# The last two rows of a decoder's last product: residual added in the PSUM bank, both parts of an input in one wide product, stores of two rows

## The chip, the cores and the metric

The kernel runs on one core of a Trainium2 chip. The metric is the device time of one execution in microseconds, the median of three runs. Engines are called TensorE (PE in the profile, with PEld for its weight loads), VectorE (DVE), ScalarE (ACT), GpSimd (POOL) and SyncE (SP).

## What is computed

A decoder of two layers on 512 tokens of width 1024 in fp32; the change touches only the very end: the down projection of the second layer's feed-forward block, the residual, and the final norm.

```python
def rms_norm(x, g):
    xf = x.astype(jnp.float32)
    y = xf * lax.rsqrt(jnp.mean(xf * xf, axis=-1, keepdims=True) + EPS)
    return (y * g.astype(jnp.float32)).astype(x.dtype)

def swiglu(h, w_gate_up, w_down):
    gu = h @ w_gate_up
    return (jax.nn.silu(gu[..., :D_FF]) * gu[..., D_FF:]) @ w_down

# in reference(), per layer and at the end:
        x = x + swiglu(rms_norm(x, ln_ffn[layer]), w_gate_up[layer], w_down[layer])
    ...
    return rms_norm(x, ln_final)
```

## The kernel before

Everything is held transposed: `self.x[m]` is one of eight rows of the residual, 128 features (the partitions) by 512 tokens. A product in nearly fp32 precision is made of three passes: each operand is split into a high and a low part (`split`, `pair`), and `mm3` issues weight-high times input-high, weight-high times input-low and weight-low times input-high into one PSUM bank. The two parts of an input are two tiles, `h` and `l`.

The feed-forward block works in two halves of 11 feature tiles. At its end `acts` holds 11 pairs of inputs, and for each row m a product of 11 times `mm3` is made over two weight pieces (`w[m][0]` of six tiles, `w[m][1]` of five), which are fetched through two buffers (`wraw`) and split by ScalarE (high) and VectorE (low). Rows 0 to 5 of the last product are 512 tokens wide: VectorE adds the bank to the residual (`add`), ScalarE squares the row, and VectorE adds the square to the running total (`accumulate`).

Rows 6 and 7 are made in the branch `if tail < KD`, for each half of the tokens apart (`parts`), so that the first half can be normed and sent while the second is still computed. The order there is: row 6 of the first half, row 7 of the first half, row 6 of the second, row 7 of the second. Ahead of them in the program, ScalarE scales rows 0 to 5 of both halves by the final gain into output tiles (`outs`, tag `T`): twelve instructions. After each of the four units VectorE adds the bank to the residual, ScalarE squares; row 6 is scaled into its output tile. `final` then sums the squares over the partitions with two products by ones (into a bank `g`), and ScalarE takes the reciprocal root twice, to the bank and to SBUF. `store` multiplies: rows 0 and 1 on GpSimd, rows 2 and 3 and then rows 4 to 6 on VectorE, row 7 on VectorE with the gain in the same instruction; each piece is sent as soon as it is done, three by SyncE's queue and rows 0 and 1 of the second half by ScalarE's.

The banks of the products rotate: `pj` has two, so row 6 of the first half takes the bank that row 4 had, and row 7 the one that row 5 had. Each engine works through its own instructions in order, and a wait holds up all that stands behind it on that engine.

Of the kernel before, what the change touches and what calls it, by code (L numbers as in the profile page):

```python
# [10 lines left out]
F32R = mybir.dt.float32r  # L11
I32 = mybir.dt.int32
AF = mybir.ActivationFunctionType
ALU = mybir.AluOpType
# [4 lines left out]
P = 128  # L19
T = 512  # L20
D = 1024
KD = D // P
# [17 lines left out]
G_MIX, G_FFN, G_KV, G_FIN = (0, 8), (16, 24), 32, 40  # L40
# [43 lines left out]
    return c  # L84


class Builder:
    def __init__(self, tc, a):
        self.tc, self.nc, self.a = tc, tc.nc, a
        self.n = 0  # L90
        self.valued, self.turned, self.scaled, self.behind = None, [], None, None
        self.scalings = []
        self.table, self.table_ins, self.table_users = None, None, []
# [67 lines left out]

    def pair(self, pool, tag=None, bufs=None):
        if tag is None:
            tag, bufs = "", KD
        return tuple(self.t(pool, [P, T], F32R, tag + p, bufs) for p in "hl")


    def split(self, src, hi, lo, eng=None):
# [27 lines left out]
    def mm3(self, ps, w, k, act, start, stop, more=False):  # L196

        (wh, wl), (ah, al) = w, act
        s = slice(k * P, (k + 1) * P)
        self.head = self.mm(ps, wh[:, s], ah, start, False, more)  # L200
        self.mm(ps, wh[:, s], al, False, False, more)
        self.last = self.mm(ps, wl[:, s], ah, False, stop, more)

    def project(self, src, acts, tag="pj", order=range(KD), w=None):
        steps = self.projected(src, acts, tag, order, w)
        return list(steps)[-1]
# [887 lines left out]
    def ffn(self, fp, xp, layer, h, apool, rope=False):  # L1094

        nc, a = self.nc, self.a
        acc = self.acc
        half = FT // 2
        acts, sums, open_pairs, places, waiting = [], [], [], [], []
# [52 lines left out]
        def add(x, ps):  # L1152
            d = ps
            if not layer:
                d = self.t(fp, [P, T], F32, "fu", 3)
                self.tt(nc.vector, d, ps, self.rstd, ALU.mult)
            self.tt(nc.vector, x, d, x, ALU.add)

        for f0 in (0, half):
# [22 lines left out]
            for m in range(tail):  # L1182
                if layer and f0 == 0:
                    self.tt(nc.vector, self.x[m], self.x[m], self.root, ALU.mult)
                ps = self.bank("pj")
                for j, n in ((0, 6), (6, 5)):
                    w = down(m, j, n)
# [7 lines left out]
        if tail < KD:  # L1195

            parts = (slice(0, T // 2), slice(T // 2, T))
            own = dict(pool=fp, tags=("T", "T"), bufs=8)
            w = {m: [down(m, j, n, **(own if m == KD - 1 else {})) for j, n in ((0, 6), (6, 5))] for m in range(tail, KD)}
            outs = [[self.t(fp, [P, D], F32, "T", 8).rearrange("p (k t) -> p k t", k=4) for _ in range(2)] for t in parts]  # L1200
            for o, t in zip(outs, parts):
                for k in range(tail):
                    self.copy(o[k // 4][:, k % 4, :], self.x[k][:, t], scale=self.gain(G_FIN, k))
            ends = []
            for t in parts:
                acc = self.acc[:, t]
                for m in range(tail, KD):
                    ps = self.bank("pj")[:, t]
                    for k in range(half):
                        self.mm3(ps, w[m][k // 6], k % 6, [x[:, t] for x in acts[k]], k == 0, k == half - 1)  # L1210
                    x = self.x[m][:, t]
                    add(x, ps)
                    sq = self.t(fp, [P, T], F32, "fg", 4)[:, t]
                    self.square(sq, x)
                    if m < KD - 1:
                        self.copy(outs[len(ends)][1][:, m % 4, :], x, scale=self.gain(G_FIN, m))
                        nxt = self.t(xp, [P, T], F32, "sqa", 2)[:, t]
                        self.tt(nc.vector, nxt, acc, sq, ALU.add)
                        acc = nxt
                ends.append(self.final(fp, (acc, sq), t))  # L1220
            for n, ((ps, r), o, t) in enumerate(zip(ends, outs, parts)):
                self.store(ps, r, o, t, n)

    def token_sums(self, fp, layer, j, h):

# [269 lines left out]
            self.fn(o, ps, AF.Abs_reciprocal_sqrt, scale=1.0 / D)  # L1495
        return to, r

    def store(self, ps, r, o, t, part):

        nc = self.nc  # L1500
        rows = self.a["out"][part]
        some = lambda k, n: o[k // 4][:, k % 4:k % 4 + n, :]
        wide = lambda f, n: f.unsqueeze(1).to_broadcast([P, n, t.stop - t.start])
        send = lambda k, n, by=nc.sync: by.dma_start(rows[:, k:k + n, :], some(k, n))
        self.tt(nc.gpsimd, some(0, 2), some(0, 2), wide(r, 2), ALU.mult)
        for k, n in ((2, 2), (4, 3)):
            self.tt(nc.vector, some(k, n), some(k, n), wide(ps, n), ALU.mult)
            send(k, n)
        self.stt(some(7, 1)[:, 0, :], self.x[7][:, t], self.gain(G_FIN, 7), ps, ALU.mult, ALU.mult)
        send(7, 1)  # L1510
        send(0, 2, nc.scalar if part else nc.sync)


def layout(i):
# [30 lines left out]
    for k in range(0, KD, 2):  # L1545
# [7 lines left out]
        "wmk": wmk[1], "wmv": wmv[1],  # L1553
        "wout": np.stack([tiles(wo[0]), tiles(o1)]),
        "wgu": np.stack([tiles(w, pair) for w in gu]),
        "wdn": np.stack([tiles(w) for w in f("w_down")]),
        "wkv": tiles(f("w_kv")),
# [18 lines left out]
```

## Time and profile before

| | |
|---|---|
| time of the runs, median | 1139.19 us (1138.91 to 1139.49) |
| profiled execution, its time | 1139.24 us |
| its span | 1137.2 us |
| granted TensorE clock | 0.999 |
| TensorE busy | 99% of the span |
| the four tail units and what follows | from 1111.17 us to the end |

The profile follows one execution. A row of the timeline has start, length, engine, line, operation, output and inputs, shape and count, and in brackets how long the engine was idle before and what ended that. Most instructions have the line of a helper: L146 is a product, L140 a ScalarE copy or scaling, L143 a square, L153 a VectorE or GpSimd operation on two tensors, L134 a function of ScalarE, L156 a VectorE operation with a scalar. Products are pipelined: the distance of two starts tells what one takes, not its length. `x12` is twelve merged instructions.

### The profile page before, as it was taken

Reading aid. Unit: us, or ns where it says so; the run is one execution under the profiler, and the core shown is the slowest. Engines: PE = TensorE matmul, PEld = TensorE weight load, DVE = VectorE, ACT = ScalarE, POOL = GpSimd, SP = SyncE. Lnnn points to the kernel's source line nnn. Section 1 sums busy time; section 2 is a strip of 40 time slices with the busy share of each in tenths; the row PEclk is TensorE's granted clock in tenths of the full one; section 3 lists DMA queues with packets and bytes.
Section 4 is the critical chain, followed back from the end, with each engine's and each line's share of the span. In section 5 each row is a group of like instructions: output and inputs, shape, how many; then the busy total and the mean of one; then the engine's idle time right before and its main releaser. Section 6 shows DMA issues by size and latency. Waiting matters only on the chain.

```text
span 1137.2 us, 19289 instructions
## 1 busy us (share of the span) xinstructions
PE 1127.4 (99%) x7337; PEld 991.3 (87%) x7337; DVE 829.0 (73%) x1542; ACT 634.1 (56%) x1271; POOL 72.8 (6%) x89
## 2 busy tenths in 40 slices
PE   9999999999999999999999999999999999999997
PEld 8888778887899988899988887788999988999986
DVE  7676976577888975588955877839999533889543
ACT  8588664566566632366643555956666322666433
POOL 0000000000011001011000000000112000111000
PEclk9999999999999999999999999999999999999999
DMA  8344352244677536378433421116677533776232
GB/s 312 116 145 149 93 130 85 84 121 148 172 163 187 142 108 176 106 178 200 126 89 101 130 74 38 56 39 194 142 203 182 141 100 105 171 191 154 78 101 86
DMA packets 71536, 151.14 MB, mean 133 GB/s; under 512 B 16861, under 2 KB 17141, under 8 KB 71445
## 3 DMA queue, kind: packets, MB, share of 16 engines
q1 hardware_dynamic: 60164, 129.21, 36.7%
q0 software_dynamic: 11136, 20.45, 11.5%
q8 instruction: 57, 0.93, 0.3%
q14 instruction: 35, 0.28, 0.1%
q10 hardware_dynamic: 144, 0.26, 0.1%
HBM read 142.94 MB, written 6.96 MB: 132 GB/s over the span
## 4 chain that ended last, share of the span: by engine, by line
PE 95%; DVE 2%; ACT 1%; DMA 1%; issue 0%; DVEq 0%; SPq 0%; ACTq 0%
PE pj L146 45%; PE g L146 38%; PE sc L146 6%; PE qk L146 3%; PE pt L146 2%; PE pt L150 1%; PE g L150 1%; DVE big L153 1%; ACT T L140 0%; DVE wlo L153 0%; DVE qv L156 0%; DVE btmp L153 0%; DMA early<-in_early 0%; ACT sm L134 0%; DMA wraw<-in_wdn 0%
## 5 line engine op out<-in xcount | busy, mean ns | idle before, releaser
L140 ACT ACTIVATE whi<-wraw 128x512 fp32r<-128x512 f32 (+3 forms) x318 | 235.9, 749 | 253.5 <-PE pj L146 167.6
L153 DVE TENSOR_TENSOR wlo<-wraw,whi 128x512 fp32r<-128x512 f32 (+3 forms) x318 | 263.3, 838 | 92.4 <-ACT whi L140 84.8
L146 PE MATMUL pj<-h,whi 128*128 128x512 f32 (+1 forms) x652 | 256.4, 395 | 0.0
L146 PE MATMUL pj<-l,whi 128*128 128x512 f32 (+1 forms) x652 | 254.4, 390 | 0.0
L146 PE MATMUL pj<-h,wlo 128*128 128x512 f32 (+1 forms) x652 | 254.1, 390 | 0.0
L146 PE MATMUL g<-T,whi 128*128 128x256 f32 x1216 | 218.5, 280 | 0.0
L146 PEld LDWEIGHTS g<-T,whi 128*128 128x128 f32 x1216 | 186.1, 188 | 1.2 <-DVE fu L156 1.2
L146 PE MATMUL g<-T,wlo 128*128 128x256 f32 x608 | 170.1, 280 | 0.0
L146 PEld LDWEIGHTS pj<-h,whi 128*128 128x128 f32 x652 | 122.4, 188 | 28.2 <-issue 4.1
L146 PE MATMUL g<-h,wlo 128*128 128x256 f32 (+1 forms) x500 | 146.1, 292 | 0.0
L146 PE MATMUL g<-l,whi 128*128 128x256 f32 (+1 forms) x500 | 146.0, 292 | 0.0
L146 PE MATMUL g<-h,whi 128*128 128x256 f32 (+1 forms) x500 | 145.6, 291 | 0.0
L146 PEld LDWEIGHTS pj<-h,wlo 128*128 128x128 f32 x652 | 122.5, 188 | 25.3 <-issue 0.9
L146 PEld LDWEIGHTS pj<-l,whi 128*128 128x128 f32 x652 | 122.8, 188 | 24.0 <-DVE l L1444 0.3
L146 PEld LDWEIGHTS g<-T,wlo 128*128 128x128 f32 x608 | 114.3, 188 | 0.0
L146 PEld LDWEIGHTS g<-l,whi 128*128 128x128 f32 x500 | 95.0, 190 | 2.0
L146 PEld LDWEIGHTS g<-h,whi 128*128 128x128 f32 x500 | 94.9, 190 | 2.0
L146 PEld LDWEIGHTS g<-h,wlo 128*128 128x128 f32 x500 | 95.1, 190 | 1.7
L1262 POOL DMA_DIRECT2D ws<-in_wgu x38 | 33.5, 881 | 741.2 <-DMA ws<-in_wgu 584.6
L140 ACT ACTIVATE whi<-ws 128x512 fp32r<-128x512 f32 x76 | 48.0, 632 | 47.1 <-PE g L146 37.8
L153 DVE TENSOR_TENSOR wlo<-ws,whi 128x512 fp32r<-128x512 f32 x76 | 52.1, 685 | 6.9 <-ACT whi L140 6.8
L1263 POOL DMA_DIRECT2D ws<-in_wgu x38 | 34.4, 906 | 194.4 <-DVE wlo L153 92.2
(399 smaller groups left out, 1681.4 us busy)
## 6 DMA issues: line engine op xcount, KB each, us to landing
wraw<-in_wgu SPq DMA_DIRECT2D x50, 512.0 KB, 4.2
ws<-in_wgu SPq DMA_DIRECT2D x76, 256.0 KB, 3.4
ws<-in_wgu POOLq DMA_DIRECT2D x76, 256.0 KB, 4.8
wraw<-in_win SPq DMA_DIRECT2D x26, 512.0 KB, 3.7
wraw<-in_wdn SPq DMA_DIRECT2D x32, 384.0 KB, 3.1
wraw<-in_wdn SPq DMA_DIRECT2D x32, 320.0 KB, 2.9
wraw<-in_wgu SPq DMA_DIRECT2D x38, 256.0 KB, 4.4
wraw<-in_wout SPq DMA_DIRECT2D x16, 512.0 KB, 3.5
```

The lines of the kernel that those rows point to most:

```text
L140: self.copied = self.nc.scalar.activation(out, in_, AF.Copy, **kw).ins
L146: return self.nc.tensor.matmul(out, lhsT, rhs, start=start, stop=stop, skip_group_check=more).ins
L150: return self.nc.tensor.transpose(out, in_, self.ident[:k, :k]).ins
L153: return eng.tensor_tensor(out=out, in0=a, in1=b, op=op).ins
L1262: nc.gpsimd.dma_start(s1, a22, accum_op=ALU.add)
L1263: nc.gpsimd.dma_start(s3, a21, accum_op=ALU.add)
```

## The change

The two parts of an input become one tile of 128 x 2 x 512 (`pair`), so that a product can read both for the same tokens. In the tail, ScalarE first copies the residual into the unit's own half of the bank. For three of the four units it also writes zeros into the other half (`clear`: ones times 0.0), and `wide` takes the weight's high part against both parts of the input in one product of 2 x 256 columns, which adds into both halves, and the weight's low part against the input's high part into the own half. Afterwards ScalarE copies the low half out, and VectorE adds it to the own half. The last unit (row 7, second half) takes the three passes of 256 columns as before, onto the residual in its bank; its square and its scaled row are read from the bank. `store` sends rows 2 and 3, 4 and 5, 6 and 7, 0 and 1, two rows each; in the second half ScalarE has scaled row 7 by its gain before, and VectorE multiplies rows 6 and 7 together.

```diff
     def pair(self, pool, tag=None, bufs=None):
         if tag is None:
-            tag, bufs = "", KD
-        return tuple(self.t(pool, [P, T], F32R, tag + p, bufs) for p in "hl")
+            tag, bufs = "hl", KD
+        both = self.t(pool, [P, 2, T], F32R, tag, bufs)
+        hl = Pair((both[:, 0, :], both[:, 1, :]))
+        hl.both = both
+        return hl
...
+    def wide(self, ps, w, k, both, stop):
+
+        (wh, wl), q = w, T // 2
+        s = slice(k * P, (k + 1) * P)
+        self.mm(ps.rearrange("p (a t) -> p a t", a=2), wh[:, s], both, False, False, True)
+        self.last = self.mm(ps[:, :q], wl[:, s], both[:, 0, :], False, stop, True)
+
+    def clear(self, ps):
+        zero = self.ones.unsqueeze(1).to_broadcast([P, ps.shape[1] // P, P])
+        self.copy(ps.rearrange("p (a t) -> p a t", t=P), zero, scale=0.0)
...
                 for m in range(tail, KD):
-                    ps = self.bank("pj")[:, t]
-                    for k in range(half):
-                        self.mm3(ps, w[m][k // 6], k % 6, [x[:, t] for x in acts[k]], k == 0, k == half - 1)
-                    x = self.x[m][:, t]
-                    add(x, ps)
+                    bank, x = self.bank("pj"), self.x[m][:, t]
+                    own, low = (bank[:, i * T // 2:(i + 1) * T // 2] for i in range(2))
                     sq = self.t(fp, [P, T], F32, "fg", 4)[:, t]
+                    self.copy(own, x)
+                    if t.start and m == KD - 1:
+                        x = own
+                        for k in range(half):
+                            self.mm3(own, w[m][k // 6], k % 6, [a[:, t] for a in acts[k]], False, k == half - 1, True)
+                    else:
+                        self.clear(low)
+                        for k in range(half):
+                            self.wide(bank, w[m][k // 6], k % 6, acts[k].both[:, :, t], k == half - 1)
+                        self.copy(sq, low)
+                        self.tt(nc.vector, x, own, sq, ALU.add)
                     self.square(sq, x)
...
         self.tt(nc.gpsimd, some(0, 2), some(0, 2), wide(r, 2), ALU.mult)
-        for k, n in ((2, 2), (4, 3)):
+        if t.start:
+            self.copy(some(7, 1)[:, 0, :], x, scale=self.gain(G_FIN, 7))
+        for k, n in ((2, 2), (4, 2), (6, 2 if t.start else 1)):
             self.tt(nc.vector, some(k, n), some(k, n), wide(ps, n), ALU.mult)
-            send(k, n)
-        self.stt(some(7, 1)[:, 0, :], self.x[7][:, t], self.gain(G_FIN, 7), ps, ALU.mult, ALU.mult)
-        send(7, 1)
+            if k < 6:
+                send(k, n)
+        if not t.start:
+            self.stt(some(7, 1)[:, 0, :], x, self.gain(G_FIN, 7), ps, ALU.mult, ALU.mult)
+        send(6, 2)
         send(0, 2, nc.scalar if part else nc.sync)
```

On ScalarE, from the last of the twelve scalings to the reciprocal roots of the first half, the program had this before (`x_523` is row 6, `x_524` row 7, `fg` a square, `T` an output tile):

```order
L140 ACTIVATE T_11682<-x_521_2729,gains_67 128x256
L140 ACTIVATE T_11682<-x_522_2730,gains_67 128x256
L143 ACTIVATE fg_11730<-x_523_2731 128x256
L140 ACTIVATE T_11680<-x_523_2731,gains_67 128x256
L143 ACTIVATE fg_11770<-x_524_2732 128x256
L134 ACTIVATE g_11774<-g_11773 128x256
L134 ACTIVATE ws_11777<-g_11773 128x256
```

And it has this now (`x_507` is row 6, `x_508` row 7; `pj_11595` is the bank of row 6 in the first half, `pj_11627` that of row 7, `pj_11664` that of row 6 in the second half):

```order
L144 ACTIVATE T_11582<-x_505_2713,gains_67 128x256
L144 ACTIVATE T_11582<-x_506_2714,gains_67 128x256
L144 ACTIVATE fg_11596<-pj_11595 128x256
L144 ACTIVATE pj_11627<-x_508_2716 128x256
L144 ACTIVATE pj_11627<-ones_69 128x256
L147 ACTIVATE fg_11596<-x_507_2715 128x256
L144 ACTIVATE T_11580<-x_507_2715,gains_67 128x256
L144 ACTIVATE pj_11664<-x_507_2715 128x256
L144 ACTIVATE pj_11664<-ones_69 128x256
L144 ACTIVATE fg_11628<-pj_11627 128x256
L147 ACTIVATE fg_11628<-x_508_2716 128x256
```

The copy of the low half of row 6 and the two writes of row 7's bank stand behind the scalings, and the writes of the second half's banks follow the square of row 6.

On TensorE, the end of row 6 and the start of row 7 in the first half read as follows before (`h`, `l` and `ac10h`, `ac10l` are the parts of inputs, `whi` and `wlo` those of row 6's weights, `T_11669` and `T_11670` those of row 7's):

```order
L146 MATMUL pj_11695<-ac10h_11345,whi_11663 128x256
L146 MATMUL pj_11695<-ac10l_11346,whi_11663 128x256
L146 MATMUL pj_11695<-ac10h_11345,wlo_11664 128x256
L146 MATMUL pj_11735<-h_10019,T_11669 128x256
L146 MATMUL pj_11735<-l_10020,T_11669 128x256
L146 MATMUL pj_11735<-h_10019,T_11670 128x256
```

And as follows now, where `hl_9930` and `ac_1663_11246` are tiles with both parts:

```order
L150 MATMUL pj_11595<-ac_1662_11243,whi_11563 128x512
L150 MATMUL pj_11595<-ac_1662_11243,wlo_11564 128x256
L150 MATMUL pj_11595<-ac_1663_11246,whi_11563 128x512
L150 MATMUL pj_11595<-ac_1663_11246,wlo_11564 128x256
L150 MATMUL pj_11627<-hl_9930,T_11569 128x512
L150 MATMUL pj_11627<-hl_9930,T_11570 128x256
```

Three products for each input have become two, the units stand in the same order, and the first product into `pj_11627` has ScalarE's zeros in `pj_11627` ahead of it.

More of the change, by code (lines that the diff above doesn't have):

```diff
@@ L84, in constants @@
     return c
+class Pair(tuple):
+    pass
 class Builder:
@@ L1219, in ffn @@
                         acc = nxt
-                ends.append(self.final(fp, (acc, sq), t))
-            for n, ((ps, r), o, t) in enumerate(zip(ends, outs, parts)):
-                self.store(ps, r, o, t, n)
+                ends.append((x, *self.final(fp, (acc, sq), t)))
+            for n, (end, o, t) in enumerate(zip(ends, outs, parts)):
+                self.store(*end, o, t, n)
     def token_sums(self, fp, layer, j, h):
@@ L1496, in final, with store @@
         return to, r
-    def store(self, ps, r, o, t, part):
+    def store(self, x, ps, r, o, t, part):
         nc = self.nc
```

## The prediction

> **What bounds the kernel now.** I read the page first, then the chain of waits over the last 48 us, then the timeline of the last 35 us engine by engine, because the change works on the last two rows of the last matrix product only. The page:
>
> ```profile
> span 1137.2 us, 19289 instructions
> PE 1127.4 (99%) x7337; PEld 991.3 (87%) x7337; DVE 829.0 (73%) x1542; ACT 634.1 (56%) x1271; POOL 72.8 (6%) x89
> PE 95%; DVE 2%; ACT 1%; DMA 1%; issue 0%; DVEq 0%; SPq 0%; ACTq 0%
> ```
>
> TensorE is busy for 99% of the span, and 95% of the chain that ended last is its own. So whatever makes TensorE wait in the tail is added to the time one for one, and whatever shortens its queue there is taken off. The chain of waits at the end, with start, length and what ran:
>
> ```profile
> 1109.36 3.05 DMA wraw<-in_wdn
> ...
> 1113.69 4.79 ACT T L140 x12
> ...
> 1121.03 7.30 PE pj L146 x61
> ...
> 1128.35 0.44 DVE x L153
> ...
> 1128.81 0.42 ACT fg L143
> ...
> 1129.28 0.71 PE g L146 x2
> ```
>
> Two things are to be seen. ScalarE has a block of its own here: the last weight piece lands at 1112.41 (1109.36 + 3.05), and behind it stand twelve scalings of finished rows. And after the last product the chain goes through a VectorE addition and a ScalarE square before TensorE can sum the squares.
>
> The four units of the tail are row 6 and row 7 of the first token half, then both of the second; I call them 6a, 7a, 6b, 7b. The timeline of TensorE has their first products, 6a at 1111.17, 7a at 1115.11, 7b at 1124.20:
>
> ```profile
> 1103.63 0.39 PE L146 MATMUL pj<-h,whi 128*128 128x512 f32 x1
> ...
> 1111.17 0.28 PE L146 MATMUL pj<-h,whi 128*128 128x256 f32 x1
> ...
> 1115.11 0.28 PE L146 MATMUL pj<-h,T 128*128 128x256 f32 x1
> ...
> 1118.94 0.28 PE L146 MATMUL pj<-ac10h,T 128*128 128x256 f32 x1
> ...
> 1119.31 0.70 PE L146 MATMUL g<-sqa,ones 128*128 128x256 f32 x2
> ...
> 1124.20 0.28 PE L146 MATMUL pj<-h,T 128*128 128x256 f32 x1
> ...
> 1128.15 0.59 PE L146 MATMUL g<-sqa,ones 128*128 128x256 f32 x2
> ...
> 1129.28 0.70 PE L146 MATMUL g<-fg,ones 128*128 128x256 f32 x2 [0.53 <-ACT fg L143]
> ```
>
> Row 5 (33 products of 512 columns) runs from 1103.63 to 1111.17, so 7.54 / 33 = 0.2285 us each; 6a (33 of 256 columns) from 1111.17 to 1115.11, so 3.94 / 33 = 0.1194 us each. 7a follows 6a without a gap: nothing outside TensorE stands between them. The same stretch on ScalarE:
>
> ```profile
> 1112.43 0.74 ACT L140 ACTIVATE T<-wraw 128x640 fp32r<-128x640 f32 x1 [2.92 <-DMA wraw<-in_wdn]
> 1113.08 0.62 ACT L143 ACTIVATE sq<-x 128x512 f32<-128x512 f32 x1
> 1113.60 4.89 ACT L140 ACTIVATE T<-x,gains 128x256 f32<-128x256 f32 x12
> 1118.39 0.40 ACT L143 ACTIVATE fg<-x 128x256 f32<-128x256 f32 x1
> 1118.70 0.50 ACT L140 ACTIVATE T<-x,gains 128x256 f32<-128x256 f32 x1
> ...
> 1121.07 0.37 ACT L134 ACTIVATE g<-g 128x256 f32<-128x256 f32 x1 [0.93 <-PE g L146]
> 1121.35 0.38 ACT L134 ACTIVATE ws<-g 128x256 f32<-128x256 f32 x1
> ...
> 1128.81 0.42 ACT L143 ACTIVATE fg<-x 128x256 f32<-128x256 f32 x1 [3.13 <-DVE x L153]
> ```
>
> ScalarE is not free before 1118.39. Today that costs nothing: its square of row 6 is wanted only by the sum at 1119.31.
>
> **The change part by part.**
>
> *The new copies ahead of 7a.* A bank must now be filled by ScalarE before TensorE adds into it: the residual into one half, zeros into the other. For 6a this is hidden:
>
> ```profile
> 1103.83 0.69 DVE L153 TENSOR_TENSOR x<-pj,x 128x512 f32<-128x512 f32 x1 [2.05 <-PE pj L146]
> ...
> 1107.73 0.74 ACT L140 ACTIVATE whi<-wraw 128x640 fp32r<-128x640 f32 x1 [2.54 <-PE pj L146]
> ```
>
> The bank it takes was row 4's, read out by VectorE until 1104.52, and ScalarE idles 2.54 us before its next weight piece there. For 7a it is not. The order of instructions shows, on ScalarE, the twelve scalings, then the copy of 6a's low half, then row 7's residual into the bank of 7a, then the zeros, and 7a's first product waits for the zeros. Nothing ahead of the scalings moves: they start behind the last weight piece, whose transfer starts at 1109.36 when VectorE has freed its buffer, as before. From 1118.39, when the scalings let the next instruction start: the copy of the low half until the next may start, 0.30 (between the 1121.07 to 1121.35 step, 0.28, and the 1118.39 to 1118.70 step, 0.31); the residual 0.40 (between 0.37 and 0.42 of the rows above), whole, since the zeros wait for its end; the zeros 0.40; two handovers of about 0.05 (1128.81 + 0.42 = 1129.23, and TensorE starts at 1129.28). That is 1118.39 + 0.30 + 0.40 + 0.05 + 0.40 + 0.05 = 1119.59. 7a starts there and not at 1115.11: **+4.48 us**. TensorE stands idle from about 1115.2 on, and everything behind 7a in its queue (the sums, 6b, 7b) waits with it. Bounds: the three copies between 0.28 and 0.50 each (0.50 is the costliest row of this size) give -0.15 to +0.35; a landing of the weight piece some 0.3 us earlier or later moves all of it.
>
> *The wide products.* For each of 11 inputs two products of 256 columns become one of 512, so 0.1194 x 3 = 0.358 becomes 0.2285 + 0.1194 = 0.348: 0.010 us an input, 0.11 us a unit. In 6a it only lengthens the idle time; in 7a and 6b it counts, 0.23 us. The rows measure 512 columns that lie together; this one reads two runs of 256. No row shows that; between nothing and 0.23 us I take 0.23, since the count of columns is the same. The Trainium skill, "TensorE: Matmul & The Clock Gate", section "Back-to-back issue gap", gives a lone product N / 2.4 ns plus 2.5 ns: by it a pair would cost 218 ns and the wide one 216 ns, 0.05 us over the two units, and the sum would be 0.2 us higher. The rows say 239 against 229 ns, and I go by them.
>
> *Between 7a and 7b.* Before, from 1115.11 to 1124.20 there are 9.09 us: 66 products at 0.1194 are 7.88, and 1.21 goes to the sums of squares. Of that 0.25 is a wait: 7a's last product starts at 1118.94, TensorE is free at 1119.06, and the sum starts at 1119.31 because the row 6 total ends at 1119.26:
>
> ```profile
> 1118.83 0.43 DVE L153 TENSOR_TENSOR sqa<-sqa,fg 128x256 f32<-128x256 f32 x1 [3.09 <-ACT fg L143]
> ```
>
> In the changed kernel that total is there long before 7a ends, so the wait goes. Late next is row 7's square: low half copied (0.38), added on VectorE (0.42), squared (0.42), with handovers some 1.5 us behind 7a's end; TensorE meets it after one sum (about 0.45) and six products of 6b (1.04), so 0 to 0.1 us of wait. 22 pairs at 0.348 are 7.65, sums 0.96, wait 0.05: 8.66 in place of 9.09, **-0.43 us**. The copies for 6b and 7b have over 2 us of cover, since ScalarE does them while 7a and 6b run.
>
> *The end of 7b.* Its products go into the bank that holds the residual, so ScalarE squares the bank directly. Before, from 1128.15 to the last sum at 1129.28 there are 1.13 us: 0.20 until VectorE starts (1128.35), the addition, then 0.47 from the square's start (1128.81) to the sum. Without the addition 0.20 + 0.47 = 0.67: **-0.46 us**. The scaling of row 7 by its gain moves to ScalarE behind the square and has the sum's 0.7 us as cover.
>
> *Four stores of two rows.* After the sum VectorE does three pieces of 512 in place of 512, 768 and 256:
>
> ```profile
> L153 DVE TENSOR_TENSOR T<-T,g 128x768 f32<-128x768 f32 x2 | 1.9, 949 | 0.0
> L153 DVE TENSOR_TENSOR T<-T,g 128x512 f32<-128x512 f32 x2 | 1.4, 687 | 3.4 <-ACT g L134 3.4
> L156 DVE SCALAR_TENSOR_TENSOR T<-x,gains,g 128x256 f32<-128x256 f32 x2 | 1.0, 476 | 0.0
> ```
>
> Three times 0.687 is 2.06 against 2.11, the last piece some 0.1 us earlier or later, with 256 KB in it and not 128. But the transfers are already full there (busy time by stretch; the last three columns are clock, DMA share, GB/s):
>
> ```profile
> 1132.00:1133.00 1.00, 0.00 (x0) 0.00 (x0) 0.36 (x1) 0.00 (x0) 0.02 (x1) 1.00 0.81 303
> 1133.00:1134.00 1.00, 0.00 (x0) 0.00 (x0) 0.00 (x0) 0.00 (x0) 0.00 (x0) 1.00 1.03 396
> 1134.00:1135.00 1.00, 0.00 (x0) 0.00 (x0) 0.00 (x0) 0.00 (x0) 0.00 (x0) 0.65 0.95 334
> ```
>
> The same megabyte goes out from about 1132.1 to 1134.9 whatever its cutting, while the first piece is as early as before. I take 0, between -0.2 and +0.2.
>
> Everything ahead of the last two rows keeps its order and its waits on all engines; a pair of tiles became one tile of the same size. Zero.
>
> **The sum** against the profiled execution (1139.24 us, its span and 2 us around it; the median of the runs is 1139.19, so the two agree): 4.48 - 0.43 - 0.46 = +3.59, so **1142.8 us**, 0.3% slower. A measurement of this kernel can tell about 0.2%, 2.3 us, from no change.
>
> **The rivals.**
>
> *The clock drops in the gap.* The changed TensorE would be idle for some 4.3 us. In the trace the granted clock falls in one place, after the last sum (1129.28 + 0.70 = 1129.98):
>
> ```profile
> 1134.20:1134.30 0.10, 0.00 (x0) 0.00 (x0) 0.00 (x0) 0.00 (x0) 0.00 (x0) 1.00 0.82 297
> 1134.30:1134.40 0.10, 0.00 (x0) 0.00 (x0) 0.00 (x0) 0.00 (x0) 0.00 (x0) 0.54 1.02 349
> ```
>
> So it fell 4.35 us into idleness, to half: the new gap is just about as long. What half costs is shown at the start of the kernel, where the first products ran out of idleness:
>
> ```profile
> 1.19 3.51 PE L146 MATMUL g<-wabs 128*128 128x256 f32 x15 [1.19 <-DVE eps L292]
> 4.54 0.28 PE L146 MATMUL pj<-mh,whi 128*128 128x256 f32 x1
> ```
>
> Fifteen of 256 columns took 3.35 us, 0.22 each against 0.119, nearly twice. About 3 us at that pace in 7a lose 1.5: 1142.8 + 1.5 = **1144.3 us**. Against it: the gap ends about when the fall came there, and the fall must come first. Chance 0.22. The Trainium skill, "TensorE: Matmul & The Clock Gate", section "Part 1: The HAM clock gate", has this as a rule: a free-running window of 3.41 us, and one idle window halves the clock. The trace agrees: 4.54 and 1134.35 lie 331 such windows apart. By it a gap of 4.3 us holds a whole window in about one execution of four ((4.3 - 3.41) / 3.41), and in the phase of this execution it would not.
>
> *The wide product gains nothing*, because two runs are read as two products: +0.23 us, **1143.0 us**. For it speaks only that no row shows it. Chance 0.06.
>
> *Not slower: TensorE does not wait for 7a.* Place: ScalarE between 1112.43 and 1118.39. If its twelve scalings were out of the way, 7a would start at 1115.0, and the change would keep its gains: -0.11 - 0.43 - 0.46 = -1.0, **1138.2 us**. It decides from the point where the zeros are written by 1115.0, 4.6 us earlier than worked out above; with 3.6 us of the wait taken away it would come out as before. Only an earlier weight piece could do it, and that transfer (3.05 us) can't start before 1109.36. Against it speaks the order on ScalarE. Chance 0.04.
>
> **How the numbers follow.** Forecast 0.68, clock 0.22, no gain from the wide product 0.06, no wait 0.04. The forecast's own range from the bounds above is 1141.7 to 1143.6 (the lower end takes copies, landing, stores and last sum all low, the upper end all high). Eight in ten must reach to the clock's case: 1141.7 to 1144.5. Faster by over 0.2% would need more than the third rival's whole gain: 0.01. Within 0.2% means under 1141.5: the third rival and the lowest tip of the forecast, 0.08. Slower 0.91.
>
> **What would show it.** On TensorE a gap of 4.2 to 4.8 us between 6a's last product and 7a's first, ended by ScalarE's write of the bank; on ScalarE that write directly behind the scalings and two copies, at about 1119.1; 7a and 6b each about 0.1 us shorter; no VectorE addition between the last product and the last square; the last stores ending as long behind the last sum as before. A gap under 2 us, or a clock below full in it, would prove the forecast wrong, as would transfers that end over 0.3 us later behind the last sum.

## The result and the profile after

The changed kernel takes 1145.02 us (median of 6 executions, 1144.29 to 1145.74), the kernel before 1139.24 (1138.91 to 1139.49): a ratio of 1.0051, with a 95% interval of 1.0038 to 1.0064. It is slower, as forecast, but by 5.8 us and not 3.6, and above the range that was given (1141.7 to 1144.5). The profiled execution is the fastest of the six: 1144.29 us with a span of 1142.2, 5.0 more than before. Its mean granted clock is 0.997, that of the others 0.995 or 0.996. In it helpers have other line numbers: L150 is a product, L144 a ScalarE copy or scaling, L147 a square, L157 a VectorE operation on two tensors.

The chain of waits of the changed kernel, with start, length and what ran, has a new piece in the tail:

```profile
1115.60 2.88 ACT T L144 x7
1118.49 0.27 ACT fg L144
1118.75 0.28 ACT pj L144
1119.03 0.02 issue
1119.06 0.40 ACT pj L144
1119.45 0.04 issue
1119.50 5.51 PE pj L150 x22
...
1133.86 0.43 PE g L150 x2
1134.29 0.04 issue
1134.33 0.71 PE g L150 x2
```

Before, TensorE went from 6a to 7a without a gap. Now the path runs over ScalarE's scalings, the copy of the low half and the two writes of row 7's bank, and only then do the 22 products of 7a start. ScalarE's second write, the zeros, starts at 1119.06, where about 1119.1 had been said. Between the last product of 7b and the last sum there is no VectorE addition any more. The timeline of TensorE:

```profile
1111.33 0.39 PE L150 MATMUL pj<-hl,whi 128*128 128x512 f32 x1
...
1115.06 0.28 PE L150 MATMUL pj<-ac,wlo 128*128 128x256 f32 x1
1119.50 4.46 PE L150 MATMUL pj<-hl,T 128*128 128x512 f32 x16 [4.15 <-ACT pj L144]
1123.80 1.21 PE L150 MATMUL pj<-ac,T 128*128 128x512 f32 x6
1124.84 0.59 PE L150 MATMUL g<-sqa,ones 128*128 128x256 f32 x2
...
1129.75 3.04 PE L150 MATMUL pj<-hl,T 128*128 128x256 f32 x24
...
1133.70 0.59 PE L150 MATMUL g<-sqa,ones 128*128 128x256 f32 x2
1134.33 0.70 PE L150 MATMUL g<-fg,ones 128*128 128x256 f32 x2
```

The gap is 4.15 us, ended by ScalarE's write. But look at 7a: its first 16 products take 4.30 us (1119.50 to 1123.80), while the 22 of 6a took 3.85 in all (1111.33 to 1115.18, which is the start of the last one, 1115.06, and the 0.12 us that it takes). The busy time by stretch says why. A row has the stretch, its length, the busy time of TensorE, its weight loads, VectorE, ScalarE and GpSimd with their instructions, and then the granted clock (the share of full speed that TensorE was given), the DMA share and GB/s:

```profile
1118.00:1119.00 1.00, 0.00 (x0) 0.00 (x0) 0.21 (x1) 1.00 (x4) 0.00 (x0) 1.00 0.00 0
1119.00:1120.00 1.00, 0.50 (x1) 0.50 (x2) 0.40 (x2) 0.97 (x4) 0.00 (x0) 0.58 0.00 0
...
1121.00:1122.00 1.00, 1.00 (x4) 0.82 (x4) 0.00 (x0) 0.00 (x0) 0.00 (x0) 0.50 0.00 0
1122.00:1123.00 1.00, 1.00 (x6) 0.88 (x5) 0.00 (x0) 0.00 (x0) 0.00 (x0) 0.72 0.00 0
1123.00:1124.00 1.00, 1.00 (x7) 0.90 (x6) 0.00 (x0) 0.00 (x0) 0.00 (x0) 1.00 0.00 0
```

In stretches of 0.1 us, at the fall and at the return:

```profile
1119.10:1119.20 0.10, 0.00 (x0) 0.00 (x0) 0.10 (x1) 0.10 (x1) 0.00 (x0) 0.76 0.00 0
...
1122.50:1122.60 0.10, 0.10 (x1) 0.06 (x1) 0.00 (x0) 0.00 (x0) 0.00 (x0) 0.68 0.00 0
```

The clock fell to half near 1119.15 (0.76 is about half a stretch at 1.00 and half at 0.50), shortly before the gap ended, and came back near 1122.56, 3.4 us later. This is the rival that the prediction gave a chance of 0.22, and a clock below full in the gap is what it had named as proof against its forecast.

Stage by stage, in this execution against that of before: 6a starts 0.16 later; from 6a's start to 7a's 8.17 in place of 3.94, +4.23; from 7a's start to 7b's 10.25 in place of 9.09, +1.16; 7b 3.95 in both; from its end to the last sum 0.63 in place of 1.13, -0.50; from there to the end of the span 7.87 in place of 7.92, -0.05. Together +5.0.

### The profile page after: what moved, and what is told of

The parts are those of the page before. It is cut to its first block, busy times and chain, and to the rows that moved or that the text cites. A ratio compares the mean times of both kernels' runs of the same rounds, so it can differ in the third digit from the quotient of the medians.

```text
span 1142.2 us, 19237 instructions
## 1 busy us (share of the span) xinstructions
PE 1128.8 (99%) x7304; PEld 991.3 (87%) x7304; DVE 828.4 (73%) x1542; ACT 637.6 (56%) x1282; POOL 73.0 (6%) x89
## 4 chain that ended last, share of the span: by engine, by line
PE 94%; DVE 3%; ACT 1%; DMA 1%; issue 0%; SPq 0%; DVEq 0%; ACTq 0%
PE pj L150 44%; PE g L150 38%; PE sc L150 6%; PE qk L150 3%; PE pt L150 2%; PE pt L154 1%; DVE big L157 1%; PE g L154 1%; DVE btmp L157 1%; DVE wlo L157 1%; ACT T L144 0%; DVE qv L160 0%; DMA early<-in_early 0%; ACT sm L138 0%; DMA big<-basein 0%
## 5 line engine op out<-in xcount | busy, mean ns | idle before, releaser
L150 PE MATMUL pj<-hl,whi 128*128 128x512 f32 x1288 | 409.0, 396 | 0.0
L144 ACT ACTIVATE whi<-wraw 128x512 fp32r<-128x512 f32 (+3 forms) x318 | 235.8, 749 | 253.3 <-PE pj L150 158.0
L157 DVE TENSOR_TENSOR wlo<-wraw,whi 128x512 fp32r<-128x512 f32 (+3 forms) x318 | 263.2, 838 | 93.7 <-ACT whi L144 86.0
L150 PEld LDWEIGHTS pj<-hl,whi 128*128 128x128 f32 x1288 | 238.5, 188 | 52.6 <-issue 4.3
L150 PE MATMUL pj<-hl,wlo 128*128 128x512 f32 (+1 forms) x652 | 253.9, 390 | 0.0
L150 PE MATMUL g<-T,whi 128*128 128x256 f32 x1216 | 218.5, 280 | 0.0
L150 PE MATMUL g<-hl,whi 128*128 128x256 f32 (+1 forms) x1000 | 193.7, 292 | 0.0
L150 PEld LDWEIGHTS g<-T,whi 128*128 128x128 f32 x1216 | 186.1, 189 | 1.2 <-DVE fu L160 1.2
L150 PE MATMUL g<-T,wlo 128*128 128x256 f32 x608 | 170.2, 280 | 0.0
L150 PEld LDWEIGHTS g<-hl,whi 128*128 128x128 f32 x1000 | 158.0, 190 | 3.9
L150 PE MATMUL g<-hl,wlo 128*128 128x256 f32 (+1 forms) x500 | 146.2, 292 | 0.0
L150 PEld LDWEIGHTS pj<-hl,wlo 128*128 128x128 f32 x652 | 122.5, 188 | 25.3 <-issue 0.9
L150 PEld LDWEIGHTS g<-T,wlo 128*128 128x128 f32 x608 | 114.4, 188 | 0.0
L150 PEld LDWEIGHTS g<-hl,wlo 128*128 128x128 f32 x500 | 95.2, 190 | 1.7
L144 ACT ACTIVATE whi<-ws 128x512 fp32r<-128x512 f32 x76 | 48.1, 633 | 46.8 <-PE g L150 38.0
L150 PE MATMUL pj<-ac,whi 128*128 128x512 f32 x186 | 58.8, 396 | 0.0
L157 DVE TENSOR_TENSOR wlo<-ws,whi 128x512 fp32r<-128x512 f32 x76 | 52.0, 685 | 6.9 <-ACT whi L144 6.8
L144 ACT ACTIVATE fs<-g 128x256 f32<-128x256 f32 x114 | 41.7, 366 | 0.7 <-PE g L150 0.6
L150 PEld LDWEIGHTS pj<-ac,whi 128*128 128x128 f32 x186 | 34.9, 188 | 8.1
```

Of the source, the lines that this page charges most:

```text
L144: self.copied = self.nc.scalar.activation(out, in_, AF.Copy, **kw).ins
L150: return self.nc.tensor.matmul(out, lhsT, rhs, start=start, stop=stop, skip_group_check=more).ins
L157: return eng.tensor_tensor(out=out, in0=a, in1=b, op=op).ins
```

## The experiments

The times of the experiments stand against the kernel before on the same chip: 1139.41 us (22 executions) for the filled gap, the bank written ahead, 9 scalings ahead and the first form of the last unit, 1139.37 (27 executions) for the others. In the edits, `nosync` only sets the order of two instructions, without a wait.

**The gap filled with products.** Between 6a and 7a, 32 products that nobody reads:

```diff
+                    if not t.start and m == KD - 1:
+                        idle = self.bank("g")[:, t]
+                        for i in range(32):
+                            ins = self.mm(idle, w[6][0][0][:, :P], acts[0][0][:, t], i == 0, i == 31)
...
```

> The changed kernel with 32 extra products of 256 columns on TensorE between row 6 and row 7 of the first half, into a bank that nobody reads: they fill 3.8 of the 4.2 us gap and change nothing else. Theory: the gap itself costs 3.5 us net and the lowered clock after it the other 2.3; with TensorE busy the clock stays full, and the time is 1142.7 us (1142.3 to 1143.1), with a granted clock of 1.00 up to the last sum. Rival, the 2.3 us come from something else (wide products, weights, transfers): the time stays at 1145.0 us.

Measured: 1142.55 us (1142.42 to 1143.14, 6 executions), a ratio of 1.0029 (1.0018 to 1.0041). TensorE's timeline and its clock, in stretches of 2 us:

```profile
1114.79 3.98 PE L150 MATMUL g<-hl,whi 128*128 128x256 f32 x32
1119.10 3.11 PE L150 MATMUL pj<-hl,T 128*128 128x512 f32 x16 [0.33 <-ACT pj L144]
```

```profile
1118.00:1120.00 2.00, 1.67 (x12) 1.36 (x11) 0.85 (x2) 1.97 (x7) 0.00 (x0) 1.00 0.02 4
1120.00:1122.00 2.00, 2.00 (x13) 1.73 (x13) 0.00 (x0) 0.44 (x2) 0.00 (x0) 1.00 0.00 0
```

From 6a's start to 7a's it is 8.17 us as in the changed kernel, but its 16 products take 2.94 us (to 1122.04) and not 4.30, at a full clock. More work on TensorE makes the kernel 2.5 us faster: the clock is worth that much in the median, and what is left, 3.1 us, is the wait less the gains. The prediction's sum for a full clock, 1142.8 or 3.6 above the kernel before, comes within half a microsecond of it.

**The bank written ahead of the scalings.** ScalarE's order written out by hand; products, additions and stores are those of the changed kernel:

```diff
-            for o, t in zip(outs, parts):
-                for k in range(tail):
-                    self.copy(o[k // 4][:, k % 4, :], self.x[k][:, t], scale=self.gain(G_FIN, k))
...
+            begin(0, KD - 2)
+            products(0, KD - 2)
+            begin(0, KD - 1)
...
+            total = finish(0, KD - 2, self.acc[:, parts[0]])
+            begin(1, KD - 2)
...
+            scaled(0)
+            products(0, KD - 1)
...
```

> The changed kernel with ScalarE's order written out: the residual and the zeros of row 7 go into its bank ahead of the twelve scalings, the scalings of the first half run while TensorE is in row 7, those of the second half while it is in the last unit. Products, additions and stores are those of the changed kernel. Theory: without the gap there is neither the wait nor the clock, and the gains stay: -0.11 -0.43 -0.46 against before, 1138.2 us (1137.9 to 1138.5). Rival, wide products or writes into the banks cost 2 us by themselves: 1140 us or more. Rival, the scalings only move the wait to the sums of squares: 1138.7 to 1139.5 us, with a gap ahead of a product by ones.

Measured: 1138.29 us (1137.79 to 1138.71, 11 executions), a ratio of 0.9991 (0.9982 to 1.0000). The timelines of ScalarE and TensorE:

```profile
1113.50 0.62 ACT L147 ACTIVATE sq<-x 128x512 f32<-128x512 f32 x1
1114.03 0.37 ACT L144 ACTIVATE pj<-x 128x256 f32<-128x256 f32 x1
1114.42 0.39 ACT L144 ACTIVATE pj<-ones 128x256 f32<-128x256 f32 x1
```

```profile
1115.25 0.28 PE L150 MATMUL pj<-ac,wlo 128*128 128x256 f32 x1
1115.37 3.00 PE L150 MATMUL pj<-hl,T 128*128 128x512 f32 x16
...
1124.01 3.04 PE L150 MATMUL pj<-hl,T 128*128 128x256 f32 x24
...
1127.96 0.59 PE L150 MATMUL g<-sqa,ones 128*128 128x256 f32 x2
1128.66 0.70 PE L150 MATMUL g<-fg,ones 128*128 128x256 f32 x2
```

The zeros are there at 1114.81, before 6a ends, and 7a follows without a gap. From 7a to 7b it is 8.64 us; 8.66 had been worked out. The gain of 1.1 us is the 1.0 that was worked out, though the interval ends just at no change. The stages show it more surely: from 7a to 7b 0.45 us less than before, from 7b's end to the last sum 0.70 in place of 1.13. The order of the same instructions on ScalarE decides between 1138.3 and 1145.0; apart from that, TensorE meets the second sum of the first half two inputs later than in the changed kernel.

**Shorter gaps.** Of the twelve scalings, 9 or 6 stay ahead of row 7's bank, the others go behind its zeros:

```diff
+            self.written = None
+            scaled(9)        # or scaled(6)
...
                     self.square(sq, x)
+                    if m == KD - 1 and not t.start:
+                        scaled(12)
```

> The changed kernel with 9 of the 12 scalings ahead of row 7's bank and 3 behind it: the gap is 1.2 us shorter, about 2.95 us. Theory that the clock falls only after a window of 3.41 us that is wholly idle: it never falls here, and the time is 1142.7 - 1.2 = 1141.5 us with little scatter. Rival, a window that is idle for the most part is enough: the clock falls in many executions still, the time is 1142 to 1144 us and scatters by 1 us or more.

> The changed kernel with 6 of the 12 scalings ahead of row 7's bank and 6 behind it: the gap is some 2.4 us shorter than in the changed kernel, about 1.7 us. The kernel with 9 ahead had a gap of 2.84 us, and the clock fell in 3 of 5 executions, 2.15 us into the gap in its profile; the changed kernel has 4.16 us and 6 of 6. Theory, estimated from these: the clock falls where a window has somewhat over 2 us of idle time in it, so never here: 1142.55 (the gap filled with products) - 2.4 = 1140.2 us (1139.8 to 1140.6), with all executions close together. Rival, any longer wait can do it: some executions above 1141.5 us.

Measured with 9 ahead: 1141.42, 1141.55, 1143.15, 1143.32 and 1145.11 us. With 6 ahead: eight executions from 1139.97 to 1140.45, three from 1142.18 to 1142.50; median 1140.34. The low groups lie where they were worked out with a full clock (1141.5 and 1140.2); the high ones are 1.7 to 3.6 and about 2.1 us above, and their mean granted clock is 0.995 to 0.997, that of the low ones 0.998 or 0.999. The gaps in the two profiles, the first of a high execution (1145.11 us), the second of a low one (1140.45 us), in which the clock stayed full from 1114 to 1121:

```profile
1118.94 5.49 PE L150 MATMUL pj<-hl,T 128*128 128x512 f32 x16 [2.84 <-ACT pj L144]
```

```profile
1117.01 3.08 PE L150 MATMUL pj<-hl,T 128*128 128x512 f32 x16 [1.80 <-ACT pj L144]
```

And the clock in the profile of the first of them, that of the execution of 1145.11 us:

```profile
1118.20:1118.30 0.10, 0.00 (x0) 0.00 (x0) 0.07 (x1) 0.10 (x1) 0.00 (x0) 0.70 0.00 0
1118.30:1118.40 0.10, 0.00 (x0) 0.00 (x0) 0.10 (x1) 0.10 (x1) 0.00 (x0) 0.50 0.00 0
...
1124.00:1125.00 1.00, 1.00 (x5) 0.89 (x4) 0.00 (x0) 0.00 (x0) 0.00 (x0) 0.50 0.00 0
1125.00:1125.10 0.10, 0.10 (x2) 0.10 (x1) 0.00 (x0) 0.00 (x0) 0.00 (x0) 0.67 0.00 0
1125.00:1126.00 1.00, 1.00 (x8) 0.89 (x6) 0.00 (x0) 0.14 (x1) 0.00 (x0) 0.97 0.00 0
```

It fell 2.1 us into the gap (the gap begins at 1116.10, the fall is near 1118.24) and stayed at half for 6.8 us, to about 1125.07. Of the 3.6 us by which this execution lies above the low ones, 2.7 are lost between 7a and 7b (11.63 against 8.89 with the gap filled); the rest lies elsewhere, as 6a starts 0.75 us later here than in the changed kernel's profile. So both theories that I put up fell in turn: that a gap must hold a wholly idle window of 3.41 us, and then that it needs over 2 us. At 1.80 us the clock fell in 3 of 11 executions, at 2.84 in 3 of 5, at 4.15 in 6 of 6. These counts are read from times and mean clocks, and in the two kernels of this experiment no execution lies between the groups; only one execution of each kernel has a profile, and its gap is taken for all. No profile shows a fall at 1.80 us.

**The gap alone.** The kernel before, with row 7's bank written twice behind the scalings and 7a made to wait for it; products, sums and stores are those of before, but one sum changes its place:

```diff
+                    if m == KD - 1 and not t.start:
+                        for scale in (1.0, 0.0):
+                            self.copy(ps, self.x[m][:, t], scale=scale)
+                            self.nosync(self.copied, scaled)
...
```

> The kernel before with the gap alone: ScalarE writes row 7's bank twice behind the scalings, square and scaling of row 6, and row 7's products of the first half (narrow, with the start flag, so what was written is overwritten) wait for that; order on TensorE as before. Theory: TensorE idles about 4.8 us, the wait of 0.25 us for the row 6 total goes, so +4.6 us, and the lowered clock adds 1.6 to 3.2: 1145.5 to 1147.0 us. Rival, the clock loss needs the wide products: 1144.0 us.

Measured: 1145.85 us (1144.63 to 1147.21, 5 executions), a ratio of 1.0057 (1.0043 to 1.0070). TensorE's timeline and the clock at the fall and at the return:

```profile
1114.75 0.28 PE L146 MATMUL pj<-ac10h,wlo 128*128 128x256 f32 x1
1118.81 1.22 PE L146 MATMUL g<-sqa,ones 128*128 128x256 f32 x2 [3.79 <-DVE sqa L153]
1119.47 0.78 PE L146 MATMUL pj<-h,T 128*128 128x256 f32 x1
```

```profile
1117.60:1117.70 0.10, 0.00 (x0) 0.00 (x0) 0.00 (x0) 0.10 (x1) 0.00 (x0) 0.80 0.00 0
...
1124.40:1124.50 0.10, 0.10 (x2) 0.10 (x2) 0.00 (x0) 0.00 (x0) 0.00 (x0) 0.56 0.00 0
```

The expectation has TensorE's order as before, but it isn't quite: the sum of the row 6 total now stands ahead of 7a, so the idle time is 3.79 us, ended by VectorE's total, and 7a starts at 1119.47. The clock was at half from about 1117.66 to 1124.49, 6.8 us. It is lost with narrow products as well; the wide ones aren't needed for it. The gap alone costs 6.5 us, and the change with it 5.8.

**The last unit alone.** As in the kernel before, three units are narrow and added by VectorE; row 7 of the second half is added onto the residual in its bank, with the stores of the change. The edit is made in the changed kernel, so each input stays one tile with both parts. In the first form that unit takes the second half of its bank, as its tokens do; the second form has `own = bank[:, :T // 2]`:

```diff
-                    self.copy(own, x)
+                    own = bank[:, t]
                     if t.start and m == KD - 1:
+                        self.copy(own, x)
                         x = own
...
                     else:
-                        self.clear(low)
...
+                            self.mm3(own, w[m][k // 6], k % 6, [a[:, t] for a in acts[k]], k == 0, k == half - 1)
+                        add(x, own)
```

> The kernel before with only the last unit and the stores of the change: row 7 of the second half adds onto the residual in its bank, its square and its scaled row are read from the bank, four stores of two rows each; the other three units are narrow products as before. Theory: the addition behind the last product goes (-0.5) and the stores cost nothing: 1138.7 us (1138.5 to 1139.0). Rival, the stores of two rows end later and give it back: 1139.2 us or more.

Measured: 1139.10 us (1138.61 to 1139.74, 11 executions), 0.9997 (0.9988 to 1.0006). This form leaves out the residual of that unit. Row 7's products of the first half begin with the start flag, in the other half of the same bank; that the first product of the second half then replaces what ScalarE wrote is read from the two forms, as no trace shows what a bank holds. With all narrow units in the first half of their banks the residual is added:

> The kernel before with only the last unit and the stores of the change, all four narrow units in the first half of their bank, so that the last one adds onto the residual. Theory: -0.5 for the addition behind the last product, stores even: 0.5 us under the kernel before. Rival, the stores give it back: even with before.

Measured: 1138.97 us (1138.35 to 1139.39, 11 executions), 0.9996 (0.9987 to 1.0005). The interval holds both no change and the expected -0.5. In the timeline of TensorE the sums show the step by itself:

```profile
1127.45 0.59 PE L150 MATMUL g<-sqa,ones 128*128 128x256 f32 x2
1128.08 0.70 PE L150 MATMUL g<-fg,ones 128*128 128x256 f32 x2
```

0.63 us where the kernel before has 1.13, so -0.50, as in the changed kernel.

**ScalarE's order alone.** The kernel before with the six scalings of each half behind the square and the scaling of its row 6:

```diff
...
+                        for k in range(tail):
+                            self.copy(outs[len(ends)][k // 4][:, k % 4, :], self.x[k][:, t], scale=self.gain(G_FIN, k))
+                            self.nosync(self.copied, squared)
```

> The kernel before with ScalarE's order alone: the six scalings of each half behind the square and the scaling of its row 6, everything else as before. Theory: only the wait of 0.25 us of the first sum for the row 6 total goes, so 0.2 to 0.3 us under before, and 0.8 us of the gain of the changed kernel with its order written out come from the wide products and the last unit. Rival, the order is most of that gain: 0.8 us or more under before.

Measured: 1139.02 us (1138.81 to 1139.62, 11 executions), 0.9998 (0.9989 to 1.0007). The medians are 0.35 apart, near the forecast, but the interval doesn't tell it from no change. Order alone (-0.35) and last unit (-0.40) leave about 0.4 of the 1.1 us for the wide products, against 0.33 worked out (11 inputs x 0.010 x 3 units). Each of these shares is within the scatter of whole executions, so the split is only suggested.

## Why the prediction was wrong

The wait and the gains were right, the total was not, and one step did it: the clock, which the sum put at nothing. Of the 1.4 us by which the profiled execution exceeds the 3.59 of the sum, 1.59 lie between 7a and 7b (+1.16 in place of -0.43); the other terms are off by less than 0.1 each.

- *Wait for row 7's bank:* worked out to end at 1119.59; it ended at 1119.50, 4.39 us after 7a's start before where 4.48 was worked out. The two writes took 0.37 and 0.39 (0.40 each was taken). Right; and the run with the bank written ahead, which has no wait, shows the cause.
- *Wide products:* two runs of 256 are read like 512 columns: 6a takes 3.85 us for 11 inputs, 0.350 each; 0.348 had been worked out, and 0.36 for three narrow ones. Right.
- *Between 7a and 7b:* 8.66 worked out; 8.64 in the kernel with the order written out, 8.89 with the gap filled, where TensorE starts 7a from a short wait; 10.25 in the changed kernel. At a full clock and without a wait the term was right. Behind a wait it was 0.23 too low: about 0.1 in the first 16 products (2.94 against 2.84) and the rest in the sums and 6b (4.90 against 4.76); the cause of these stays open.
- *End of 7b:* -0.46 worked out, -0.50 measured. *Stores:* 0 worked out, -0.05 measured. The first stores of two rows go out as early as before, and the span ends as long after the last sum.
- *The clock:* the step that failed, in "the gap ends about when the fall came there, and the fall must come first". I read one fall, 4.35 us into idleness, as the idle time that a fall needs, and gave the case 0.22 and 1.5 us. But 4.35 us was what happened to pass in that execution. In profiles the clock fell 2.1 us into a gap of 2.84 and 3.8 us into the gap of 4.15, and by times and mean clocks in 3 of 11 executions with a gap of 1.80 us. With 4.15 us it fell in six of six. It costs 1.4 us where it stays at half for 3.4 us (10.25 against 8.89 from 7a to 7b) and 2.7 where it stays for 6.8 us (11.63, from 1118.94 to 1130.57, with 9 scalings ahead). So the price of 1.5 was right for one such stretch: the rival's 1144.3 is the time of the profiled execution, where errors of some 0.2 us both ways cancel by luck. But the median of the changed kernel is 2.5 above the filled gap, and the mean clocks of the other five, 0.995 or 0.996, suggest that most of them had two stretches; none of these was profiled. The lost clock belonged in the sum and not among the rivals; its price of 2.5 is known only from these runs.
- The prediction's sentence on the Trainium skill ("TensorE: Matmul & The Clock Gate", section "Part 1: The HAM clock gate") made it look safer: by one wholly idle window of 3.41 us, a gap of 2.84 or 1.80 could never lower the clock, and one of 4.3 would do it in about one execution of four. The runs decide against that reading: all six executions of the changed kernel lost the clock, and in the profile with 9 scalings ahead TensorE was idle for only 2.1 of the last 3.4 us before the fall. The length of the window fits what was seen: half speed lasted 3.4 or 6.8 us.

What stays open is the exact rule. An estimate from the counts: if activity is judged by windows of 3.4 us whose place against the gap is chance, a window that is idle for about half is enough to explain all three. One with some 0.7 us of idle time at its start (1118.24 to 1118.94) kept the clock low for another. Neither was measured by itself.

## What to carry to other kernels

A product that adds onto data written by another engine waits for all that stands ahead of the write in that engine's queue; look at what that is, and put the write ahead of work that nobody waits for. A wait of TensorE of about 2 us or more must be priced with the clock that it can lose, here 1.4 to 2.7 us on top of the wait; filling it with products that nobody reads won that back here. A step whose gain is 0.5 us of 1139 can be shown in the timeline (0.63 against 1.13 us) where the times of whole executions can't tell it.

## What the hardware showed that was not expected

- TensorE's clock falls in gaps well under 3.4 us: in the profile 2.1 us into a gap of 2.84, and by times and mean clocks in 3 of 11 executions at 1.80 us, 3 of 5 at 2.84, 6 of 6 at 4.15.
- Once low, it stayed at half for one stretch of 3.4 us (1119.15 to 1122.56) or two (1118.24 to 1125.07, and with the gap alone 1117.66 to 1124.49), though TensorE was busy again after 0.35, 0.7 and 1.15 us.
- What ScalarE writes into a bank is added to or replaced, depending on the products that ran in that bank before. The two forms of the last unit differ in this alone: after a start flag in the other half of the bank the residual was lost, and where the same columns had been written since the flag it was added. The Trainium skill, "PSUM — Partial Sum Buffer", section "The four PSUM rules", says the same of a seed other than zero.
